# Low parts of the split weights: from a subtraction on VectorE to a negation on ScalarE and an accumulating DMA

## Chip, cores, metric

The kernel runs on one NeuronCore of one Trainium2 chip. The metric is the device time of one launch in microseconds, the median of several runs.

## What is computed

A two-layer decoder trunk on 512 tokens of 1024 channels in float32: one wide input projection, four token mixers (sparse attention NSA, stick-breaking, gated linear attention GLA, forgetting attention FoX), gated branch projections and an output projection, then a feed-forward part with a squared ReLU, and a last norm.

```python
proj = h @ w_in                                   # h = RMSNorm(x), 1024 -> all mixers and gates
ys = jnp.stack([y_nsa, y_sb, y_gla, y_fox], axis=2)
branch = jnp.einsum('bsnc,ncd->bsnd', ys, w_branch)
gates = jax.nn.sigmoid((gate_logits + b_gate).astype(jnp.float32)).astype(x.dtype)
mixed = jnp.sum(gates.reshape(B, S, N_BRANCH, D_MODEL) * branch, axis=2)
x = x + mixed @ w_out
h2 = rms_norm(x, norm_ff)
return x + jnp.square(jax.nn.relu(h2 @ w_ff1)) @ w_ff2
```

## The kernel before

All activations stay on the core, channels on the 128 partitions and the 512 tokens along the row. The weights stream in from device memory in chunks of 128x1024 float32 (512 KB): 350 in the program, in the order in which they are used (`in_w[i]`).

A matrix product is made of three products of a shorter float format (float32r). A weight chunk W is split into a high part `wh` (W rounded to float32r) and a low part W - `wh`; the activations are split likewise into `xh` and `xl`. PE then sums wh*xh + wl*xh + wh*xl. `mtile` (and its kin `mhalves`, `vproducts`) does this: 24 matmuls per chunk, and the second one already uses the low part.

`chunk` (lines 265 to 277) makes the operands. SP loads the chunk into one of three buffers `wr0` to `wr2` (line 271). ACT copies it, rounded, to `wh`, of which there are two buffers (line 275). DVE subtracts `wh` from the raw chunk and writes the low part over the raw chunk (line 276). A `wr` buffer appears under two names: `wr0f` read or written as float32, `wr0r` as float32r. 334 chunks are split this way, 167 per layer: 95 in the mixers, 8 in the output projection, 64 in the feed-forward part. The other 16 (8 per layer, in NSA's compression) are used as they come.

So a `wr` buffer is loaded anew once PE has used the chunk three places earlier, and a `wh` buffer is written anew once PE has used the chunk two places earlier.

In the mixers (some 736 us per layer) a list, `MIXERS`, sets the order in which the pieces of projections and attention are written down, and a scheduler orders the instructions of each engine from there. Attention work lies between the projections' matmuls on PE; POOL does masks (`AFFINE_SELECT`, lines 633 and 713), rotations (line 827) and the sum into `mixed` (line 536). Then comes the output projection (line 465), and the feed-forward part: four groups of 8 chunks that make the hidden tiles (first half: DVE scales by the norm in line 475, ACT squares and rounds in lines 476 and 478, DVE makes the low part in line 479) and 8 chunks that add into `x` (second half, DVE in line 485). Every matmul is recorded at line 121. PSUM tiles are `pd` for the mixers' projections and `ps` elsewhere.

Of the kernel before, what the change touches and what calls it, by code (L numbers as in the profile page):

```python
# [32 lines left out]
# columns of the per-layer small pack  # L33
# [3 lines left out]
# columns of the constant pack  # L37
# [10 lines left out]
class Dual:  # L48
    """a buffer seen as float32 and as float32r"""
# [14 lines left out]
class Kern:  # L64
# [117 lines left out]
    def setup_more(self):  # L182
# [24 lines left out]
        # second-pass key operands: rows 0-63 keys, then rows of -1 (64-95 or 96-127), zeros elsewhere  # L207
# [17 lines left out]
        # rope tables, rows as channels of two heads  # L225
# [29 lines left out]
    def order(self, a, b):  # L255
        """b after a on their engine"""
        self.tc.add_manual_dep(b.ins, a.ins.name,
                               mybir.DependencyInfo(mybir.DependencyClass.NoSync, mybir.DependencyReason.DATA),
                               reason="table order")
# [5 lines left out]
    def chunk(self, split=True):  # L265
        nc = self.nc
        i = self.cidx
        self.cidx += 1
        with self.tc.high_priority(4000 if i == 0 else 2000):
            raw = self.dual("wr")  # L270
            nc.sync.dma_start(raw.f[:], self.A["w"][i])
            if not split:
                return raw.f[:]
            wh = self.t("wh", 1024, F32R)
            nc.scalar.activation(wh[:], raw.f[:], AF.Copy)  # L275
            nc.vector.tensor_sub(raw[:], raw.f[:], fb(wh[:]))  # L276
        return wh, raw

    def mtile(self, xh, xl):
        """one tile of 128 output channels, transposed: [128 ch, 512 tok] in PSUM"""  # L280
        wh, wl = self.chunk()
        o = self.ps(self.dtag)
        n = len(xh)
        for k in range(n):
            s = slice(k * P, (k + 1) * P)
            self.mm(o[:], wh[:, s], xh[k][:], k == 0, False)
            self.mm(o[:], wl[:, s], xh[k][:], False, False)
            self.mm(o[:], wh[:, s], xl[k][:], False, k == n - 1)
        return o

    def mhalves(self, xh, xl):
        """mtile by halves of the tokens: (PSUM, tokens)"""
        wh, wl = self.chunk()
        for h in range(2):
            t = slice(h * 256, h * 256 + 256)
            o = self.ps(self.dtag, 256)
            for k in range(KT):
                s = slice(k * P, (k + 1) * P)
                self.mm(o[:], wh[:, s], xh[k][:, t], k == 0, False)
                self.mm(o[:], wl[:, s], xh[k][:, t], False, False)  # L300
                self.mm(o[:], wh[:, s], xl[k][:, t], False, k == KT - 1)
            yield o, t

    def vproducts(self, bank):
        """256 channels, token-major: two banks of two token tiles"""
        acc = [self.ps(bank) for _ in range(2)]
        for half in range(2):
            wh, wl = self.chunk()
            for k in range(4):
                for t in range(4):  # L310
                    o = acc[t // 2][:, (t % 2) * 256:(t % 2) * 256 + 256]
                    kk = half * 4 + k
                    s = slice(k * 256, (k + 1) * 256)
                    ts = slice(t * P, (t + 1) * P)
                    self.mm(o, self.hh[kk][:, ts], wh[:, s], kk == 0 and t % 2 == 0, False)
                    self.mm(o, self.hl[kk][:, ts], wh[:, s], False, False)
                    self.mm(o, self.hh[kk][:, ts], wl[:, s], False, kk == 7)
        return acc

    def vtiles(self, evac, acc=None):  # L320
        """evac(tok tile, psum [128 tok, 256 ch]) of the next 256 channels"""
        acc = acc or self.vproducts("d")
        with self.hi():
            for t in range(4):
                evac(t, acc[t // 2][:, (t % 2) * 256:(t % 2) * 256 + 256])

# [1 line left out]
    def rms(self, x, bank, early, in_psum=False):  # L328
        """x tiles -> 1/rms per token: [128, 512] (rows alike) and token-major [128, 4]"""
# [33 lines left out]
    def norm_split(self, x, gcol):  # L363
        """x * g as two parts; the tokens' 1/rms goes onto what is made of them"""
        nc = self.nc
        HH, HL = [], []
        for k in range(KT):
            hh, hl = self.hsplit(k)
            g = gcol[:, k:k + 1]
            nc.scalar.activation(hh[:], x[k][:], AF.Copy, scale=g)  # L370
            nc.vector.scalar_tensor_tensor(hl[:], x[k][:], g, fb(hh[:]), OP.mult, OP.subtract)
            HH.append(hh)
            HL.append(hl)
        return HH, HL

    def scaled(self, dst, o, scale=1.0):
        """dst = o * scale / rms"""
# [3 lines left out]
    def final(self, x):  # L381
        """the last norm; the last tile of channels comes in two halves of the tokens"""
# [36 lines left out]
    def layer(self, l, x):  # L419
# [5 lines left out]
        # the first products need no norm before they are written out  # L425
# [25 lines left out]
        # output projection  # L451
# [36 lines left out]
    def ysplit(self, y):  # L488
        """y [128, 512] -> (high, low) tiles; the low part takes y's place"""
# [6 lines left out]
    def sigmoid(self, z):  # L496
        """in place, z at least -44"""
# [5 lines left out]
    def branch(self, n, qt):  # L503
        """mixed += sigmoid(gate_n + b) * (y_n @ W_branch_n), two tiles of channels"""
# [34 lines left out]
    def qk_pair(self, b_tiles=None):  # L539
        """project a pair of heads; per head (A, Q1, Q2) with  # L540
        head 0: A=[kh;kl], Q1=[qh;qh], Q2[0:64]=ql; head 1: A=[kl;kh], Q1=[qh;qh]; with b_tiles
        (rows 0-63 = kh) ql in Q2[0:64], else in the rows of kh"""
# [16 lines left out]
    def kstack(self, k, A, B, b):  # L559
        """k on rows b*64..: its high part there in A, the low part in A's other half"""  # L560
# [7 lines left out]
    def regions(self, S3, win):  # L568
        """per key block: (psum AP, first query)"""
# [13 lines left out]
    def rowmax(self, S3, dst, win, negc=None):  # L583
        """column maxima of the masked scores; dst [32 rows, 512] gets diag(m)"""
# [35 lines left out]
    def probs(self, S3, win=False, bias=None, strict=False):  # L620
        """exp of the scores, masked; list of (AP, first query) per key block"""
# [19 lines left out]
    def pv(self, o, V, pr, start=True):  # L641
        """o [M, 512] += V_j^T P_j"""
# [3 lines left out]
    def recip(self, s, rows):  # L646
        """1/s for s [64 rows of PSUM], written at `rows`"""
# [7 lines left out]
    def v_plain(self, tag, c):  # L655
        """256 channels of values, token-major"""
# [6 lines left out]
    def sb_v(self, c, acc):  # L663
        """values of four heads, each as its high and low parts beside each other"""
# [17 lines left out]
    def sb_att(self, i):  # L682
        """scores with the queries on partitions, so that the sums over later keys are scans"""
# [3 lines left out]
        for b in range(2):  # L687
# [5 lines left out]
            # rows of 128 queries against all keys up to them: (bank, first column)  # L693
# [30 lines left out]
            # keys on partitions: (bank, first column) of a block of keys, queries from the same block on  # L724
# [27 lines left out]
    def vpair_evac(self, V, pair0):  # L752
        """token tile of 256 channels (4 heads) into [V0 | 1 | V1] groups of 192"""
# [15 lines left out]
    def small_proj(self):  # L769
        """nsa gates rows 0-23, gla decay rank rows 32-47, forget gate rows 64-71"""  # L770
# [16 lines left out]
        # gates of the three parts of the sparse attention, through DRAM to be read as rows alike  # L787
# [31 lines left out]
    def rope(self, o, scale, r=None):  # L819
        """rotated o * scale / rms, in r or in a tile of its own"""  # L820
# [11 lines left out]
    def compress_in(self, pecol):  # L832
        """two tiles [128 = (two positions, channel), 8 position pairs, 64 = (group, 31 blocks + pe)]"""
# [22 lines left out]
    def cmp_step(self, i, c):  # L856
        """a quarter of the first compression product"""
# [14 lines left out]
        if c == 3:  # L872
            # the position part
# [74 lines left out]
    def nsa(self, pi):  # L948
        """selected (here: all causal) and window attention of two heads"""
        nc = self.nc  # L950
        g, q, Ab, V = pi // 2, self.q, self.Ab, self.vnsa
        if True:
# [3 lines left out]
            for b in range(2):  # L956
# [7 lines left out]
                for br in range(2):  # L964
# [7 lines left out]
                    # [V|1] or [1|V] by the half the group's values sit in  # L972
# [17 lines left out]
    def nsa_cmp(self, g):  # L990
        """compressed attention of group g's four heads"""
# [40 lines left out]
    def gla_x(self, n, i):  # L1032
        """q (scaled) or k of two heads"""
# [7 lines left out]
    def gla_b(self, i):  # L1041
        """decays of two heads, summed within 64 tokens"""
# [25 lines left out]
    def gla(self, i):  # L1068
# [4 lines left out]
        if True:  # L1073
# [3 lines left out]
            # far pairs: products of decays from the middle of 512, 256 and 128 tokens  # L1077
# [47 lines left out]
            # pairs of one block of two tokens, the diagonal with them  # L1125
# [17 lines left out]
            # the other levels inside a block of 128 tokens; the two heads' queries beside each other,  # L1143
            # each with zeros at the other's channels
# [61 lines left out]
    def logsig(self, z, out):  # L1206
        """out = min(z, 0) - ln(1 + exp(-|z|))"""
# [10 lines left out]
def _kxm(w, c0):  # L1218
    """[K, 128 columns] -> [128, K/128 * 128]"""
    k = w.shape[0] // P  # L1220
    return w[:, c0:c0 + P].reshape(k, P, P).transpose(1, 0, 2).reshape(P, k * P)
# [9 lines left out]
# the token mixers' pieces in the order they are emitted: projections (with weights) and, in steps, attention  # L1231
# [142 lines left out]
```

## Time and profile before

| | |
|---|---|
| median of 3 runs | 2278.51 us (2278.09 to 2279.06) |
| span of the profiled execution | 2273.7 us |
| busy: PE, DVE | 2230.2 us (98%), 1488.2 us (65%) |
| busy: ACT, POOL | 1035.6 us (46%), 428.5 us (19%) |
| DMA traffic | 204.75 MB, mean 90 GB/s |

The profiled execution's span, from its first to its last instruction, is 2273.7 us; the runs' times are some 4.8 us longer. A matmul's row lasts 0.39 us, yet matmuls start every 0.23 us: they are pipelined, so starts tell the beat, and "busy" of PE can hide short waits. PEld is the load of a matmul's weights and runs beside the matmul before it. An idle time in brackets in a timeline names what ended it.

### The profile page before, as it was taken

The page shows a single profiled execution, that of the slowest core. Times are in us where ns is not written, and L with a number is a line of the kernel's source. Part 1 is how long each engine was busy: PE and PEld are TensorE (multiplying, and loading weights), DVE is VectorE, ACT ScalarE, POOL GpSimd, SP SyncE. Part 2 cuts the span into 40 slices and gives each one's busy share as a digit, 9 for nine tenths or more (in the row PEclk, how much of TensorE's full clock was granted, in tenths as well). Part 3 has the DMA queues.
Part 4 walks back from the last instruction along what each step waited for, and adds up shares of the span by engine and source line. Part 5 has one row for each costly group of instructions (what it writes and reads, how often), then busy time and mean ns, then how long its engine had stood idle before and what let it go on. Part 6 is the DMA issues. An engine that isn't in the chain of part 4 may idle for free.

```text
span 2273.7 us, 28986 instructions
## 1 busy us (share of the span) xinstructions
PE 2230.2 (98%) x10740; PEld 1824.9 (80%) x10740; DVE 1488.2 (65%) x2434; ACT 1035.6 (46%) x1663; POOL 428.5 (19%) x759
## 2 busy tenths in 40 slices
PE   8999999999899999999999999999989999999998
PEld 7888878887788888888888888788868888888886
DVE  6889687888875444343458886978888654344344
ACT  5775544445544333232347654534454443232233
POOL 1223024434211200000112220234431112000000
PEclk9999999999999999999999999999999999999999
DMA  4222223322124332333432222233211243333332
GB/s 164 77 72 68 90 68 96 113 79 79 47 67 128 103 93 93 95 99 94 125 105 69 66 75 85 74 98 118 76 56 58 83 130 93 94 99 95 93 94 92
DMA packets 63108, 204.75 MB, mean 90 GB/s; under 512 B 7496, under 2 KB 10184, under 8 KB 62968
## 3 DMA queue, kind: packets, MB, share of 16 engines
q1 hardware_dynamic: 62968, 202.90, 29.1%
q8 instruction: 86, 1.41, 0.3%
q14 instruction: 54, 0.44, 0.1%
HBM read 198.57 MB, written 4.29 MB: 89 GB/s over the span
## 4 chain that ended last, share of the span: by engine, by line
PE 91%; DVE 5%; issue 1%; DMA 1%; ACT 1%; POOL 1%; POOLq 0%; DVEq 0%; SPq 0%; ACTq 0%
PE ps L121 48%; PE pd L121 42%; PE ps L730 1%; DMA wr1f<-in_w 0%; DMA wr0f<-in_w 0%; DVE sh L844 0%; POOL sm L613 0%; DVE wr1r L276 0%; DVE Q L616 0%; DVE m L1214 0%; DVE m L591 0%; DVE sx L609 0%; DVE m L605 0%; DVE Q L1109 0%; ACT wh L275 0%
## 5 line engine op out<-in xcount | busy, mean ns | idle before, releaser
L121 PE MATMUL pd<-hh,wh 128*128 128x512 f32 x1040 | 415.8, 400 | 0.2 <-ACT wh L275 0.2
L121 PE MATMUL pd<-hl,wh 128*128 128x512 f32 x1040 | 407.8, 392 | 0.0
L275 ACT ACTIVATE wh<-wr1f 128x1024 fp32r<-128x1024 f32 x112 | 118.7, 1060 | 274.7 <-PE ps L121 175.0
L275 ACT ACTIVATE wh<-wr0f 128x1024 fp32r<-128x1024 f32 x111 | 117.6, 1060 | 265.4 <-PE ps L121 176.3
L121 PEld LDWEIGHTS pd<-hh,wh 128*128 128x128 f32 x1040 | 195.6, 188 | 50.0 <-issue 4.0
L275 ACT ACTIVATE wh<-wr2f 128x1024 fp32r<-128x1024 f32 x111 | 117.6, 1060 | 256.9 <-PE ps L121 172.7
L121 PEld LDWEIGHTS pd<-hl,wh 128*128 128x128 f32 x1040 | 195.5, 188 | 42.2 <-issue 0.5
L121 PE MATMUL ps<-hh,wh 128*128 128x512 f32 x512 | 201.3, 394 | 0.0
L121 PE MATMUL ps<-hl,wh 128*128 128x512 f32 x512 | 199.3, 389 | 0.0
L276 DVE TENSOR_TENSOR wr0r<-wr0f,wh 128x1024 fp32r<-128x1024 f32 x111 | 143.4, 1292 | 43.0 <-ACT wh L275 42.5
L485 DVE TENSOR_TENSOR x<-x,ps 128x512 f32<-128x512 f32 (+1 forms) x65 | 44.2, 679 | 191.7 <-PE ps L121 191.7
L276 DVE TENSOR_TENSOR wr2r<-wr2f,wh 128x1024 fp32r<-128x1024 f32 x111 | 144.5, 1302 | 35.0 <-ACT wh L275 34.8
L121 PE MATMUL pd<-hh,wr2r 128*128 128x512 f32 x392 | 156.6, 400 | 0.0
L276 DVE TENSOR_TENSOR wr1r<-wr1f,wh 128x1024 fp32r<-128x1024 f32 x112 | 138.1, 1233 | 28.2 <-ACT wh L275 27.7
L475 DVE SCALAR_TENSOR_TENSOR p<-ps,rb 128x512 f32<-128x512 f32 x64 | 43.9, 691 | 157.3 <-PE ps L121 149.2
L121 PE MATMUL ps<-v,wh 128*128 128x512 f32 (+1 forms) x392 | 135.8, 389 | 0.0
L121 PE MATMUL pd<-hh,wr1r 128*128 128x512 f32 x336 | 134.4, 400 | 0.0
L121 PE MATMUL pd<-hh,wr0r 128*128 128x512 f32 x312 | 124.6, 399 | 0.0
L121 PE MATMUL ps<-p,v 128*128 128x384 f32 (+3 forms) x384 | 116.1, 426 | 2.2 <-POOL p L633 2.2
L121 PEld LDWEIGHTS ps<-hh,wh 128*128 128x128 f32 x512 | 96.1, 188 | 24.6 <-issue 0.5
L121 PE MATMUL pd<-yh,wh 128*128 128x512 f32 x256 | 105.0, 410 | 9.9 <-ACT yh L492 9.0
L121 PEld LDWEIGHTS ps<-hl,wh 128*128 128x128 f32 x512 | 96.2, 188 | 21.3
(638 smaller groups left out, 5326.8 us busy)
## 6 DMA issues: line engine op xcount, KB each, us to landing
wr0f<-in_w SPq DMA_DIRECT2D x117, 512.0 KB, 3.6
wr1f<-in_w SPq DMA_DIRECT2D x117, 512.0 KB, 3.6
wr2f<-in_w SPq DMA_DIRECT2D x116, 512.0 KB, 3.6
G<-gd SPq DMA_DIRECT2D x48, 128.0 KB, 3.1
x<-in_x SPq DMA_DIRECT2D x16, 256.0 KB, 3.5
xs<-x SPq DMA_DIRECT2D x8, 256.0 KB, 3.7
x<-xs SPq DMA_DIRECT2D x8, 256.0 KB, 3.3
out_y<-p SPq DMA_DIRECT2D x8, 256.0 KB, 2.4
```

The costliest lines, as they stand in the source:

```text
L121: i = self.nc.tensor.matmul(o, l, r, start=start, stop=stop, skip_group_check=True)
L275: nc.scalar.activation(wh[:], raw.f[:], AF.Copy)
L276: nc.vector.tensor_sub(raw[:], raw.f[:], fb(wh[:]))
L475: nc.vector.scalar_tensor_tensor(r[:], o[:], 0.0, self.rb[:], OP.max, OP.mult)
L485: nc.vector.tensor_add(x[m][:, h], x[m][:, h], o[:])
L730: nc.tensor.transpose(S3[n][:, c:c + P], at(F, q)[:, j * P:(j + 1) * P], self.ident)
```

## The change

The subtraction on DVE goes. ACT writes the negated high part, -`wh`, over the raw chunk (new line 277), and a DMA issued from POOL adds the same chunk of weights from device memory onto it (new line 278): -`wh` + W. The rest of the diff only blanks comments and docstrings, so that lines behind move by two.

```diff
@@ class Kern, chunk() @@
             wh = self.t("wh", 1024, F32R)
             nc.scalar.activation(wh[:], raw.f[:], AF.Copy)
-            nc.vector.tensor_sub(raw[:], raw.f[:], fb(wh[:]))
+
+            nc.scalar.activation(raw[:], fb(wh[:]), AF.Copy, scale=-1.0)
+            nc.gpsimd.dma_start(raw[:], self.A["w"][i].bitcast(F32R), accum_op=OP.add)
         return wh, raw
```

Two places show how the engines' orders move. First ACT, in the first half of the last feed-forward group: `wh` is a chunk's high part, `p` the hidden tile, `v` its rounded high part. Before:

```order
L275 ACTIVATE wh_17453<-wr2f 128x1024
L476 ACTIVATE p_17409<-p_17409 128x512
L478 ACTIVATE v_2216_17412<-p_17409 128x512
L275 ACTIVATE wh_17489<-wr0f 128x1024
L476 ACTIVATE p_17445<-p_17445 128x512
L478 ACTIVATE v_2221_17448<-p_17445 128x512
```

and with the change:

```order
L275 ACTIVATE wh_17738<-wr1f 128x1024
L478 ACTIVATE p_17693<-p_17693 128x512
L277 ACTIVATE wr1r<-wh_17738 128x1024
L480 ACTIVATE v_2211_17696<-p_17693 128x512
L275 ACTIVATE wh_17775<-wr2f 128x1024
L478 ACTIVATE p_17730<-p_17730 128x512
L277 ACTIVATE wr2r<-wh_17775 128x1024
L480 ACTIVATE v_2216_17733<-p_17730 128x512
```

The negation (L277) stands behind the square of a hidden tile (L476 before, L478 now), and the rounding behind the negation.

On POOL, in the stick-breaking pieces of layer 0's mixers (`e0f` to `e5f` are tiles of scores being masked, `qk` a rotated projection). Before:

```order
L713 AFFINE_SELECT e0f<-e0f 128x128
L713 AFFINE_SELECT e1f<-e1f 128x128 x2
L713 AFFINE_SELECT e2f<-e2f 128x128
L713 AFFINE_SELECT e0f<-e0f 128x128
L713 AFFINE_SELECT e1f<-e1f 128x128 x2
L713 AFFINE_SELECT e2f<-e2f 128x128
L827 TENSOR_TENSOR qk_1910<-qk_1910,Sn 128x512
```

and with the change:

```order
L715 AFFINE_SELECT e0f<-e0f 128x128
L715 AFFINE_SELECT e1f<-e1f 128x128 x2
L715 AFFINE_SELECT e0f<-e0f 128x128
L715 AFFINE_SELECT e1f<-e1f 128x128 x2
L278 DMA wr2r<-in_w 128x1024
L715 AFFINE_SELECT e2f<-e2f 128x128
L278 DMA wr0r<-in_w 128x1024
L715 AFFINE_SELECT e2f<-e2f 128x128
L278 DMA wr1r<-in_w 128x1024
L829 TENSOR_TENSOR qk_1932<-qk_1932,Sn 128x512
L278 DMA wr2r<-in_w 128x1024
```

Each adding DMA (L278) has taken a place among the masks, in one queue with them. POOL's list has 342 rows more than before (860 for 518), ACT's 335 more, DVE's 336 fewer, and PE's and SP's as many as they had.

## Rows read from the trace of the kernel before

**Rows 1.** Spans and granted TensorE clock of the cores.

```profile
core 0: 2273.7 us, clock 0.991
```

**Rows 2.** Busy time by stretch: us, busy (xinstructions) per engine, PE clock, DMA share, GB/s.

```profile
core 0: us, PE busy (x) PEld busy (x) DVE busy (x) ACT busy (x) POOL busy (x), PEclk, DMA share, GB/s
300.00:500.00 200.00, 198.74 (x998) 161.47 (x997) 163.91 (x332) 87.29 (x155) 78.63 (x160) 1.00 0.29 89
500.00:700.00 200.00, 189.41 (x922) 151.53 (x921) 159.94 (x287) 100.72 (x168) 50.10 (x68) 0.97 0.23 71
1000.00:1100.00 100.00, 100.00 (x435) 81.46 (x434) 39.78 (x45) 29.04 (x36) 0.00 (x0) 1.00 0.31 97
1400.00:1600.00 200.00, 198.56 (x998) 162.45 (x997) 160.99 (x324) 94.22 (x166) 74.53 (x153) 1.00 0.31 93
1600.00:1800.00 200.00, 189.53 (x921) 149.89 (x920) 167.05 (x310) 96.46 (x164) 55.62 (x87) 0.97 0.21 65
```

**Rows 3.** Chain of waits, two of its longest pieces: start us, us, what.

```profile
671.86 64.25 PE pd L121 x278
...
798.22 344.80 PE ps L121 x1520
```

**Rows 4.** Timeline of PE, first half of the feed-forward part: start us, us, instruction.

```profile
2004.86 0.39 PE L121 MATMUL ps<-hh,wh 128*128 128x512 f32 x1
...
2010.40 0.39 PE L121 MATMUL ps<-hh,wh 128*128 128x512 f32 x1
2010.41 0.19 PEld L121 LDWEIGHTS ps<-hh,wr2r 128*128 128x128 f32 x1
```

**Rows 5.** Timeline of ACT and DVE in the same stretch.

```profile
2005.06 1.06 ACT L275 ACTIVATE wh<-wr2f 128x1024 fp32r<-128x1024 f32 x1 [3.30 <-PE ps L121]
2006.15 1.23 DVE L276 TENSOR_TENSOR wr2r<-wr2f,wh 128x1024 fp32r<-128x1024 f32 x1 [0.40 <-ACT wh L275]
...
2006.67 0.63 ACT L478 ACTIVATE v<-p 128x512 fp32r<-128x512 f32 x1
```

**Rows 6.** Costliest groups, line 276: busy us, mean ns, idle before, what ended it.

```profile
L276 DVE TENSOR_TENSOR wr0r<-wr0f,wh 128x1024 fp32r<-128x1024 f32 x111 | 143.4, 1292 | 43.0 <-ACT wh L275 42.5
...
L276 DVE TENSOR_TENSOR wr1r<-wr1f,wh 128x1024 fp32r<-128x1024 f32 x112 | 138.1, 1233 | 28.2 <-ACT wh L275 27.7
```

**Rows 7.** View of line 276: who waited for it (us, times).

```profile
  PEld pd L121: 3.4, 8
  PE pd L121: 0.8, 2
  PEld ps L121: 0.3, 1
  PE ps L121: 0.3, 1
```

**Rows 8.** Timelines of PE, ACT and DVE, second half of the feed-forward part.

```profile
2049.25 0.39 PE L121 MATMUL ps<-v,wh 128*128 128x512 f32 x1
...
2049.45 1.06 ACT L275 ACTIVATE wh<-wr1f 128x1024 fp32r<-128x1024 f32 x1 [1.95 <-PE ps L121]
...
2050.54 1.22 DVE L276 TENSOR_TENSOR wr1r<-wr1f,wh 128x1024 fp32r<-128x1024 f32 x1 [0.41 <-ACT wh L275]
```

**Rows 9.** DMA: a queue's share; median us to landing; an issue in SP's timeline.

```profile
q1 hardware_dynamic: 62968, 202.90, 29.1%
...
wr0f<-in_w SPq DMA_DIRECT2D x117, 512.0 KB, 3.6
...
G<-gd SPq DMA_DIRECT2D x48, 128.0 KB, 3.1
...
2004.82 0.33 SPq L271 DMA_DIRECT2D wr0f<-in_w  x1
```

**Rows 10.** Waits, one of them: total us, times, longest.

```profile
ACT wh L275 <- PE pd L121: 230.5, 104, 5.4
```

**Rows 11.** Busy time by stretch where PE waits in the mixers (columns as rows 2).

```profile
570.00:580.00 10.00, 4.88 (x20) 3.72 (x18) 9.70 (x18) 7.89 (x15) 4.81 (x4) 0.76 0.00 0
580.00:590.00 10.00, 8.33 (x45) 6.90 (x46) 9.21 (x16) 3.11 (x5) 4.44 (x4) 0.73 0.18 52
```

## Prediction

> **What bounds the kernel now.** The table of spans [rows 1] gives 2273.7 us for the profiled execution at a granted clock of 0.991; the median of the runs is 2278.51, so I add 4.8 us for what lies around the span. The table by stretches [rows 2] says who is busy: from 1000 to 1100 us, in the feed-forward part, PE is busy all the time, DVE 40% and ACT 29%, POOL not at all. In the mixers PE is still at 189 to 199 of 200 us, and DVE at 160 to 167. The chain of waits [rows 3] has the same two faces: one unbroken piece of 344.80 us of PE for the feed-forward part of layer 0 (layer 1 has its like), and in the mixers many pieces of PE, the longest 64.25 us. So PE's matmuls set the time, and anything that PE doesn't wait for is free. The question is whether PE will wait for the new low parts.
>
> The timeline of PE [rows 4] gives the beat. A chunk is 24 matmuls; one begins at 2004.86 and the next at 2010.40, so P = 5.54 us. The second matmul of a chunk already uses the low part, and its weights are loaded at 2010.41. The same chunk's high part is made by ACT at 2005.06, right after the chunk two places earlier has ended at 2004.86, since there are two `wh` buffers, and DVE's low part is done at 2006.15 + 1.23 = 2007.38 [rows 5]: 3.0 us early. That spare time is what the change spends.
>
> **What goes away.** 334 subtractions on DVE, 143.4 us for the 111 of one buffer and 138.1 us for the 112 of another [rows 6], with the third's 144.5 some 426 us in all. In the feed-forward part DVE is not waited for, so this returns nothing there. The low part held up PE's matmuls and weight loads 12 times for 4.8 us in all [rows 7]. In the mixers a freer DVE can give back some of PE's idle time: in the four stretches of rows 2 it is 1.26 + 10.59 + 1.44 + 10.47 = 24 us. Nothing bounds it below but zero, all of it is the upper end, and I take half: **-12 us**.
>
> **What is added on ACT.** 334 negations of 128x1024. ACT's row of the same shape has 1.06 us, so 354 us; ACT is at 29 to 50% in rows 2, and carries the sum. But the negation stands in the path to the low part. In the second half of the feed-forward part a chunk ends at 2049.25, ACT starts the high part at 2049.45, and what read it before started at 2050.54 [rows 8]; the negation starts there and ends at 2051.60, which is 2.35 us after the chunk's end. In the first half the square of the hidden tile stands between the two on ACT (the order of ACT shows it): after the 2005.06 of the high part the next free place is 2006.67 [rows 5], so the negation ends at 2007.73, 2.87 us after the chunk's end. The low part must be there 2010.41 - 2004.86 = 5.55 us after that end. What is left for the transfer is **5.55 - 2.35 = 3.2 us** in the second half and in the output projection, and **5.55 - 2.87 = 2.7 us** in the first half.
>
> **What the accumulating DMA takes, A.** From the end of the negation to the low part's arrival: a hop to POOL, POOL's issue, the transfer with its addition. The trace has no DMA from POOL and none that adds. Low end: a plain load of the same 512 KB takes 3.6 us from issue to landing, median [rows 9]. High end: twice that, 7.2, as if the old value were fetched by a transfer and the sum written by another. Between: the old value has to be read as well, 512 KB more. The hardware queue's packets took 29.1% of 2273.7 us, that is 662 us for 202.90 MB, or 1.7 us for one chunk [rows 9]; 3.6 + 1.7 = 5.3. POOL's issue and the hop I put at 0.7, twice the 0.33 that SP's issue shows [rows 9]. So A = 6.0, nearer to the loads than to two of them in a row, with 3.6 and 7.2 as ends. The Trainium skill, page Collectives: The Full Stack, section The bandwidth ceiling, says that a reducing transfer needs two source reads where a copy needs one, and runs at half the copy's rate for that; with the first read alone A would be 4.3, and the sum below about 200 us smaller. No row here shows it yet.
>
> Even the plain load's 3.6 us misses both places. A lateness of x is paid once in two chunks, not in each: chunk j+2 is late against chunk j, and the chunk between follows j+2 in the same stride. So the loss per chunk is (A - 3.2)/2 or (A - 2.7)/2.
>
> **Feed-forward part and output projection.** Two layers have 2 x (32 + 8) = 80 chunks of the first kind and 64 of the second. 80 x 1.4 + 64 x 1.65 = 112 + 106 = **+218 us**. At A = 3.6 it is 80 x 0.2 + 64 x 0.45 = 45; at 7.2, 160 + 144 = 304.
>
> **Mixers.** 190 chunks, 95 in a layer, in about 736 us (the output projection begins where the 64-us piece that starts at 671.86 ends) [rows 3]. That is 7.7 us per chunk against 5.54, since matmuls of the attention stand between; where they do, the low part has time. In stretches like the 64.25 us (278 matmuls, 11.6 chunks on end) it has none. Working the other way, ACT's high parts here waited for PE's last reader 104 times for 230 us [rows 10], so the ring of two is tight here too; and ACT and POOL serve in order. On POOL the adding DMA waits at the queue's head for ACT, with the attention's masks, rotations and `mixed` sums behind it, which ACT and PE wait for in their turn; and it stands itself behind masks that wait for ACT or DVE. I take half of the 1.4: 190 x 0.7 = **+133 us**. Ends: none of it at A = 3.6 (the attention covers 0.4), 190 x 1.0 = 190 at A = 7.2. SP's loads are moved nowhere: chunk j+3 is still loaded when chunk j ends, lands 3.6 us later, and is needed a chunk later still. The wire carries 334 x 0.52 MB more, 1.7 us of a beat of 5.5, over a share of 0.31 [rows 2]; room enough.
>
> **Sum.** 2273.7 + 218 + 133 - 12 = 2612.7 against the profiled execution; with 4.8 around it, **2618 us**. Changes under 0.2% (4.6 us) count as none.
>
> **Rivals.**
> *A plain load's price.* If adding costs the wire nothing, A lies in 3.6 to 4.8: +45 - 12 and some mixers at the one end, 80 x 0.8 + 64 x 1.05 + 190 x 0.4 - 12 = 195 at the other: 2320 to 2474. For it speaks that the load moves at full width already; against it, that the old value must come from somewhere.
> *PE's clock falls, or the add is slower than 7.2.* The stall of a pair of chunks lies in one piece, about 3 us at A = 6. Where PE stood idle 5 of 10 us, from 570 on, the granted clock was 0.76 and 0.73 in two stretches [rows 11], a mixture of its levels of 1.2 and 2.4 GHz. Losing a quarter of the rate over a pair's 14 us costs 3.5 us, or 1.75 per chunk: 144 x 1.75 = 252, giving 2870. The Trainium skill, page TensorE: Matmul & The Clock Gate, section HAM oscillation, has waits for transfers between bursts of matmuls slow each burst anew; by that rule this rival would hold. Against it: 580 to 590 follows a much emptier stretch. And at A = 9: 80 x 2.9 + 64 x 3.15 + 190 x 1.45 = 709, less 12, giving 2976.
> *Faster.* If the low part arrives within 2.7 us of the negation's end, the feed-forward part loses nothing, and the mixers return up to the 24 us: 2278.5 - 24 = 2255. DVE's load of over 80% in rows 2 is for it. Against it: 2.7 is under the shortest plain load of this size, and under the 3.1 us of one of a quarter of the size [rows 9].
> *The change doesn't do what it says* falls out: the order has 334 negations on ACT, 334 DMAs on POOL and no subtraction of weights on DVE.
>
> **Chances.** Forecast (A from 4.8 to 7.2 with the clock kept, 2474 to 2761) 0.50; plain price 0.15; slower still 0.25; faster 0.06; no change 0.04. The range 2350 to 2930 leaves out faster and no change (0.10), a corner of the plain price (0.02) and the worst of the slow cases (0.08). Slower 0.90, same 0.04, faster 0.06.
>
> **What would show it.** In the feed-forward stretch a chunk should begin every 6.9 to 7.2 us instead of 5.54, with PE waiting in every second chunk at its first low-part matmul for a DMA that POOL issued; that DMA's row should read about 5 us from issue to landing. DVE should fall by 426 us, ACT rise by 354. If PE's beat there stays at 5.54, the transfer fits in 2.7 us and the forecast is wrong in its main term; if PE waits for ACT or a mask rather than for the low part, the mixers' term is.

## The result, and the profile after

The changed kernel takes **2764.34 us** (median of 3 runs, 2762.99 to 2773.08) against 2278.51: **1.2145 times as long, interval 1.2119 to 1.217**. The forecast was 2618 with a range of 2350 to 2930; the sign and the main mechanism held, and the size fell 146 us short of the time. The forecast's own case, an adding transfer of at most 7.2 us with the clock kept, ended at 2761; that the range held the result by a wide margin it owes to the rival of the clock.

First the table of spans (as [rows 1]): the profiled execution grew by 487.5 us, and the granted clock fell.

```profile
core 0: 2761.2 us, clock 0.952
```

If the clock is always at one of its two levels, 2.4 and 1.2 GHz (full and half), a mean of 0.952 means 2 x 0.048 x 2761.2 = 265 us at half clock, where before had 2 x 0.009 x 2273.7 = 41.

The view of DMA (as [rows 9]) shows the new queue and its transfers; the last number of an issue's row is the median from issue to landing.

```profile
q0 software_dynamic: 48096, 175.13, 39.2%
q1 hardware_dynamic: 62968, 202.90, 22.9%
...
wr0f<-in_w SPq DMA_DIRECT2D x117, 512.0 KB, 3.7
...
wr1r<-in_w POOLq DMA_DIRECT2D x112, 512.0 KB, 5.6
```

The adds move less than the loads, and take more of the 16 DMA engines: 0.392 x 2761.2 / 334 = 3.24 us for a chunk, against 1.6 us for a loaded one, worked out in the same way.

Now the timelines in the first half of the feed-forward part, as [rows 4, 5], for one chunk. ACT:

```profile
1050.62 1.06 ACT L275 ACTIVATE wh<-wr1f 128x1024 fp32r<-128x1024 f32 x1 [4.12 <-PE ps L121]
1051.58 0.61 ACT L478 ACTIVATE p<-p 128x512 f32<-128x512 f32 x1
1052.10 1.04 ACT L277 ACTIVATE wr1r<-wh 128x1024 fp32r<-128x1024 f32 x1
1053.05 0.62 ACT L480 ACTIVATE v<-p 128x512 fp32r<-128x512 f32 x1
1057.61 1.06 ACT L275 ACTIVATE wh<-wr2f 128x1024 fp32r<-128x1024 f32 x1 [3.94 <-PE ps L121]
```

POOL:

```profile
1053.44 0.86 POOL L278 DMA_DIRECT2D wr1r<-in_w  x1 [6.29 <-ACT wr1r L277]
```

PE:

```profile
1057.41 0.40 PE L121 MATMUL ps<-hh,wh 128*128 128x512 f32 x1
1059.04 0.47 PE L121 MATMUL ps<-hh,wr1r 128*128 128x512 f32 x1 [1.23 <-ACT wh L275]
1059.34 0.40 PE L121 MATMUL ps<-hl,wh 128*128 128x512 f32 x1
```

The negation ends at 1053.14, the add's row starts 0.30 later, and this transfer lands at 1058.94, after 5.5 us; PE takes up the first low product at 1059.04. The bracket there names ACT's high part, but that row (the first of ACT's) had ended at 1051.68: a wait for several semaphores is put down to one of them, and the time shows that it was the transfer. The others are alike: all 182 first low products for which PE stood idle over 0.15 us (79 in the mixers, 103 behind them) start 0.04 to 0.09 us after their own chunk's add has landed. PE's chunk takes 1057.61 - 1050.62 = 6.99 us by ACT's starts, instead of 5.54. A wait costs a little more than its bracket: from 1057.41 to 1059.04 are 1.63 us where the beat is 0.23, and the next start comes 0.07 late too, so 1.47 for a bracket of 1.23, or 0.24 on top in this wait.

PE's idle time before matmuls that read a low part is grouped by operand (`pd` the mixers' tiles, `ps` here the first half's of the feed-forward part; busy us, mean ns, idle before). In the same six groups before, it was 0.0.

```profile
L121 PE MATMUL pd<-hh,wr2r 128*128 128x512 f32 x392 | 166.8, 426 | 46.7 <-DMA wr2r<-in_w 14.5 <-ACT wh L275 9.3 <-issue 6.6
L121 PE MATMUL pd<-hh,wr1r 128*128 128x512 f32 x336 | 139.7, 416 | 29.1 <-DMA wr1r<-in_w 8.6 <-ACT wh L275 8.5 <-issue 4.7
L121 PE MATMUL pd<-hh,wr0r 128*128 128x512 f32 x312 | 129.4, 415 | 25.0 <-DMA wr0r<-in_w 14.3 <-ACT wh L275 4.5 <-ACT A L565 3.0
...
L121 PE MATMUL ps<-hh,wr1r 128*128 128x512 f32 x176 | 73.4, 417 | 25.1 <-ACT wr2r L277 12.1 <-ACT p L478 6.6 <-ACT wh L275 4.8
L121 PE MATMUL ps<-hh,wr0r 128*128 128x512 f32 x168 | 70.3, 418 | 26.2 <-ACT wr1r L277 13.3 <-ACT p L478 7.2 <-ACT wh L275 5.0
L121 PE MATMUL ps<-hh,wr2r 128*128 128x512 f32 x168 | 70.1, 417 | 25.7 <-ACT p L478 6.9 <-ACT v L480 5.9 <-ACT wr0r L277 4.2
```

Summed over all groups that read a low part, by their place on PE's timeline, this is 138 us in 85 waits in the mixers and 175 us in 109 waits in the output projection and feed-forward part.

Last the stretches (columns as [rows 2]): two of the mixers, and the output projection with the feed-forward part of each layer.

```profile
300.00:500.00 200.00, 178.22 (x750) 139.36 (x751) 99.29 (x216) 98.13 (x147) 63.88 (x127) 0.94 0.59 130
500.00:700.00 200.00, 179.58 (x899) 144.05 (x898) 128.63 (x299) 102.61 (x175) 84.55 (x148) 0.92 0.54 124
854.10:1378.90 524.80, 432.60 (x1741) 332.38 (x1740) 85.51 (x125) 200.41 (x243) 81.23 (x87) 0.97 0.68 148
2209.90:2761.20 551.30, 446.85 (x1798) 346.13 (x1797) 93.90 (x149) 203.57 (x248) 76.40 (x84) 0.94 0.65 142
```

DVE is relieved as foreseen (99 for 164 us in the first, where PE gets through 750 matmuls and not 998), PE waits everywhere, and the clock is below 1 in all four. In this table and below, a layer is cut where ACT starts the first high part (L275) of the output projection (the layer's 96th split chunk) and where the next layer begins. "Mixers" is what lies before the first cut, "rest" (output projection and feed-forward part) what lies behind it; both are summed over the two layers of the profiled execution, in us. The times of e3, e4, e5, e7, e8 and e9 are of one run each, the others medians of several.

| kernel | time | mixers | rest |
|---|---|---|---|
| before | 2278.51 | 1453 | 821 |
| the change | 2764.34 | 1685 | 1076 |
| low products last (e1) | 2394.68 | 1517 | 876 |
| before, low products last (e2) | 2299.46 | 1474 | 824 |
| change in the mixers only (e3) | 2518.72 | 1692 | 824 |
| change in the rest only (e4) | 2561.35 | 1454 | 1105 |
| copying instead of adding (e5) | 2488.72 | 1563 | 924 |
| before, ACT's high part twice (e6) | 2341.37 | 1493 | 845 |
| waits filled with matmuls (e7) | 2749.97 | 1673 | 1075 |
| change in the rest, 3 `wh` buffers (e8) | 2491.22 | 1517 | 972 |
| later waits filled (e9) | 2728.52 | 1674 | 1052 |
| four chunks a layer only (e10) | 2279.63 | 1457 | 821 |
| before, a POOL DMA per chunk (e11) | 2276.96 | 1458 | 821 |
| before, no low part (e12) | 2263.72 | 1443 | 817 |

The mixers lost 232 us and the rest 255. The kernel before took 2274.2 to 2277.1 us beside these runs.

### The profile page after: what moved, and what is told of

It is laid out like the page before. It is cut to its first block, busy times and chain, and to the rows that moved or that the text cites. A ratio compares the mean times of both kernels' runs of the same rounds, so it can differ in the third digit from the quotient of the medians.

```text
span 2761.2 us, 30120 instructions
## 1 busy us (share of the span) xinstructions
PE 2374.7 (86%) x10740; PEld 1884.3 (68%) x10740; DVE 1080.7 (39%) x2100; ACT 1354.6 (49%) x1997; POOL 676.1 (24%) x1093
## 4 chain that ended last, share of the span: by engine, by line
PE 65%; DMA 11%; issue 10%; ACT 9%; DVE 4%; POOL 1%; POOLq 0%; SPq 0%; DVEq 0%; ACTq 0%
PE ps L121 33%; PE pd L121 32%; ACT wh L275 4%; DMA wr0r<-in_w 3%; DMA wr2r<-in_w 2%; DMA wr1r<-in_w 2%; DMA wr0f<-in_w 1%; DMA G<-gd 1%; ACT wr0r L277 1%; ACT wr2r L277 1%; DMA wr2f<-in_w 1%; ACT wr1r L277 1%; ACT hh L372 0%; PE ps L732 0%; DMA wr1f<-in_w 0%
## 5 line engine op out<-in xcount | busy, mean ns | idle before, releaser
L121 PE MATMUL pd<-hh,wh 128*128 128x512 f32 x1040 | 427.6, 411 | 4.6 <-ACT wh L275 3.1
L121 PE MATMUL pd<-hl,wh 128*128 128x512 f32 x1040 | 423.7, 407 | 0.0
L275 ACT ACTIVATE wh<-wr1f 128x1024 fp32r<-128x1024 f32 x112 | 118.7, 1060 | 370.4 <-PE ps L121 220.9
L275 ACT ACTIVATE wh<-wr2f 128x1024 fp32r<-128x1024 f32 x111 | 117.7, 1060 | 343.4 <-PE ps L121 224.6
L275 ACT ACTIVATE wh<-wr0f 128x1024 fp32r<-128x1024 f32 x111 | 117.6, 1059 | 342.9 <-PE ps L121 219.6
L121 PEld LDWEIGHTS pd<-hl,wh 128*128 128x128 f32 x1040 | 204.8, 197 | 43.8 <-issue 1.7
L278 POOL DMA_DIRECT2D wr1r<-in_w x112 | 97.4, 870 | 536.4 <-ACT wr1r L277 512.0
L278 POOL DMA_DIRECT2D wr2r<-in_w x111 | 96.7, 871 | 476.8 <-ACT wr2r L277 454.5
L121 PE MATMUL pd<-hh,wr2r 128*128 128x512 f32 x392 | 166.8, 426 | 46.7 <-DMA wr2r<-in_w 14.5
L278 POOL DMA_DIRECT2D wr0r<-in_w x111 | 96.8, 872 | 444.4 <-ACT wr0r L277 440.1
L121 PE MATMUL ps<-v,wh 128*128 128x512 f32 (+1 forms) x392 | 144.3, 411 | 8.2 <-ACT wh L275 8.2
L121 PEld LDWEIGHTS pd<-hh,wr2r 128*128 128x128 f32 x392 | 78.1, 199 | 72.5 <-DMA wr2r<-in_w 15.8
L277 ACT ACTIVATE wr1r<-wh 128x1024 fp32r<-128x1024 f32 x112 | 118.3, 1056 | 1.8
```

The source lines that it names most:

```text
L121: i = self.nc.tensor.matmul(o, l, r, start=start, stop=stop, skip_group_check=True)
L277: nc.scalar.activation(raw[:], fb(wh[:]), AF.Copy, scale=-1.0)
L278: nc.gpsimd.dma_start(raw[:], self.A["w"][i].bitcast(F32R), accum_op=OP.add)
```

## The experiments

### Is it the low part's lateness?

**e1**, the change with the low products of a chunk behind its high ones, so that the low part is due 16 matmuls later; `mhalves`, `vproducts` and the branch products alike. **e2** is the same order without the change.

```diff
@@ def mtile() @@
             self.mm(o[:], wh[:, s], xh[k][:], k == 0, False)
-            self.mm(o[:], wl[:, s], xh[k][:], False, False)
-            self.mm(o[:], wh[:, s], xl[k][:], False, k == n - 1)
+            self.mm(o[:], wh[:, s], xl[k][:], False, False)
+        for k in range(n):
+            s = slice(k * P, (k + 1) * P)
+            self.mm(o[:], wl[:, s], xh[k][:], False, k == n - 1)
```

> The changed kernel, with PE's matmuls of a chunk in another order: its 16 high-part products first, its 8 low-part products last. Theory (the low part's 5.9 us from the negation's end is what PE waits for): the low part is now needed 16 x 0.23 = 3.7 us into the chunk, and the high buffer is free 8 x 0.23 = 1.8 us before the chunk's end, so the room for the transfer grows from 2.7 to 3.2 us to over 8 us; feed-forward part and output projection return from 1076 to 821 us, and the mixers give back most of their 232 us: 2280 to 2320 us. Rival (in the mixers it is ACT's and POOL's fuller queues, whatever the low part's date): feed-forward part back, mixers not: about 2510 us. Rival (PE's clock keeps the loss): no such quick return, over 2600 us.

> The kernel before with the same new order of PE's matmuls, as a control: DVE's low part was 3.0 us early in the feed-forward part, so a later need gains nothing there; theory: 2278 us within 0.5%. If the new order by itself were worth something in the mixers (the high buffers free earlier), it shows here, up to 24 us.

e1 took 2394.68 us, 1.053 (1.0514 to 1.0546) of before, e2 2299.46, 1.0111 (1.0094 to 1.0128). The control e2 is itself a small miss: it was expected within 0.5% of before, and lost 21 us in the mixers. The new order gives back 370 of the 486 us. It moves the low part's due date, and also frees the high part's buffer 8 matmuls earlier; either way the path has more room, so most of the loss is the wait for the low part. The rest is not nothing: e1 stays 95 us above e2, which was not expected. Some 78 of them are still waits for low parts, and the transfers point to why these come later (view of DMA, then of the stretch 1000 to 1100):

```profile
q0 software_dynamic: 48096, 175.13, 44.1%
...
wr1f<-in_w SPq DMA_DIRECT2D x117, 512.0 KB, 4.1
...
wr1r<-in_w POOLq DMA_DIRECT2D x112, 512.0 KB, 7.0
```

```profile
1000.00:1100.00 100.00, 97.20 (x419) 77.95 (x418) 17.96 (x26) 45.61 (x50) 15.33 (x18) 1.00 0.84 184
```

Once PE's beat is back near 5.9 us, the DMA engines are at 0.84, the add lands after 6.6 to 7.0 us and the load after 4.1 to 4.2, and ACT's high part waits for loads:

```profile
ACT wh L275 <- DMA wr0f<-in_w: 156.3, 59, 8.3
```

**e5**, the change with a copy in place of the add.

```diff
-            nc.gpsimd.dma_start(raw[:], self.A["w"][i].bitcast(F32R), accum_op=OP.add)
+            nc.gpsimd.dma_start(raw[:], self.A["w"][i].bitcast(F32R))
```

> The changed kernel with POOL's DMA copying the chunk instead of adding it: the sum is left out, so the low part is replaced by the whole weight. Theory (the add costs a second read, 1.5 to 1.7 us on the wire): from issue to landing about 4.0 us instead of 5.6, so A is 4.3; by the prediction's terms the loss falls from 487 to about 487 - 200 = 290 us or less: 2450 to 2560 us. Rival (the price is POOL's way of issuing, and the add is free): landing 5.6 us as now and 2764 us.

It took 2488.72 us:

```profile
q0 software_dynamic: 48096, 175.13, 24.5%
...
wr1r<-in_w POOLq DMA_DIRECT2D x112, 512.0 KB, 3.9
```

So the addition itself costs 5.6 - 3.9 = 1.7 us of the path, and 276 us of the time. On the DMA engines the copy takes 0.245 x 2487.0 / 334 = 1.82 us for a chunk, the add 3.24. The rest shrank by 152 us: 144 chunks x 1.7 / 2 = 122 by the prediction's rule, and the time at half clock there fell from 98 to 24 us.

**e8**, the change in the rest only, with a third `wh` buffer (`r` and `qk` give one up), to break the rule that a lateness is paid every second chunk.

```diff
-    TAGS = dict(wh=(2, 1024), yh=(5, 512), gt=(2, 512), v2=(4, 512), v3=(4, 768), A=(5, 512), Q1=(3, 512),
-                Q2=(2, 512), m=(2, 512), r=(3, 512), p=(4, 512), sh=(3, 512), sm=(5, 64), sx=(6, 16), ng=(4,
-                32), bc=(6, 1), rb=(1, 512), rt=(1, 4), hid=(1, 256), qk=(3, 512), G=(2, 512))
+    TAGS = dict(wh=(3, 1024), yh=(5, 512), gt=(2, 512), v2=(4, 512), v3=(4, 768), A=(5, 512), Q1=(3, 512),
+                Q2=(2, 512), m=(2, 512), r=(2, 512), p=(4, 512), sh=(3, 512), sm=(5, 64), sx=(6, 16), ng=(4,
+                32), bc=(6, 1), rb=(1, 512), rt=(1, 4), hid=(1, 256), qk=(2, 512), G=(2, 512))
```

> The accumulating DMA in the output projection and feed-forward part alone (2561 us, 1105 us there), with three buffers for the high part; two tags that the mixers use give up one buffer each for the room. Theory (two high buffers put the whole path between the end of one chunk and the second next): the path may now take two chunks; what binds next is the ring of three raw buffers, load 3.9 + two ACT passes and square 2.7 + 5.9 to 7.3 us + the chunk's 5.3, over three: 5.9 to 6.4 us a chunk, 144 of them 850 to 920 us: about 2310 to 2390 us. Rival (the wire is full): 7 us a chunk stays.

A miss: 2491.22 us. The rest fell from e4's 1105 to 972 us, but to no less, and the new buffer counts cost the mixers 63 us against e4. ACT hardly waits for PE's last reader of `wh` any more, but for loads:

```profile
ACT wh L275 <- DMA wr0f<-in_w: 257.9, 92, 8.1
```

A `wr` buffer now goes through load (4.1, median in the rest), high part and negation (2.1), add (6.7) and PE's use (5.5) before it can be loaded again: 18.4 us for three buffers is a beat of 6.1 at least, by these medians; the rest's mean is 972 / 144 = 6.75. The next ring behind the one relieved was as short.

### Where, and what else the change brings

**e3** and **e4**, the change in one part of each layer alone (`i % 175 < 103` and `>= 103`), DVE subtracting elsewhere.

```diff
+            if i % 175 < 103:
                 nc.scalar.activation(raw[:], fb(wh[:]), AF.Copy, scale=-1.0)
                 nc.gpsimd.dma_start(raw[:], self.A["w"][i].bitcast(F32R), accum_op=OP.add)
+            else:
+                nc.vector.tensor_sub(raw[:], raw.f[:], fb(wh[:]))
```

> The accumulating DMA for the mixers' chunks alone; in the output projection and the feed-forward part DVE subtracts as before. Theory (each part pays for itself): 2764 - 255 = 2509 us. Rival (the feed-forward part's loss comes from elsewhere, as from the clock): above 2600 us.

> The accumulating DMA for the chunks of the output projection and the feed-forward part alone. Theory: 2764 - 232 = 2532 us, a beat of 7.0 to 7.5 us per chunk there, mixers as before at 731 and 722 us. Rival (the mixers' loss spills over): another sum.

2518.72 and 2561.35 us: each part loses by itself. The mixers lose the same as in the whole (1692 for 1685), the rest 29 us more (1105 for 1076), for which the clock answers below.

**e6**, before with ACT's high part made twice, for the longer work on ACT.

```diff
+            nc.scalar.activation(wh[:], raw.f[:], AF.Copy, scale=-1.0)
             nc.scalar.activation(wh[:], raw.f[:], AF.Copy)
```

> The kernel before (DVE subtracts), with one more ACT pass over each chunk: ACT writes the negated high part into the high buffer and then the high part over it, 334 x 1.06 us more on ACT and both parts 1.1 us later. Theory (ACT has room, the date of the low part is what counts and DVE is early by more than that): 2275 to 2310 us. Rival (the mixers lose by ACT's fuller queue): 2400 us or more, with the feed-forward part unchanged at 5.54 us a chunk.

A miss: 2341.37 us, 1.0291 (1.0274 to 1.0308). It delays the high part by 1.06 us, which the change does not; still it shows that 1.06 us of delay on this path costs 66 us, of them 40 in the mixers. As much work on ACT as the change adds thus cost the mixers 40 us here, delay included, where the change cost them 232.

**e11**, before with a DMA of 4 KB per split chunk on POOL, which waits for ACT as the change's does.

```diff
             nc.vector.tensor_sub(raw[:], raw.f[:], fb(wh[:]))
+            nc.gpsimd.dma_start(self.t("dm", 8, F32R)[:], wh[:, 0:8])
```

> Edit: the kernel before, DVE subtracting as ever, and one more DMA per split chunk, issued from POOL, that waits for ACT's high part like the change's DMA does and copies 8 columns of it to a tile that nobody reads. It brings the change's place at the head of POOL's queue and POOL's issue, without any wait of PE for a transfer. Theory (the mixers lose by the late low parts and by the clock, not by POOL's masks and sums standing behind the DMAs): 2274 to 2285, mixers 731 to 735 us a layer against 730.6 and 722.4. Rival (POOL's order is a good part of the 232 us that the mixers lost): 2320 or more, mixers 750 or more, PE waiting for masks or for the branch sums.

2276.96 us, 1.0 (0.9991 to 1.001). POOL issued 334 of them, and the time did not move: in a kernel where PE does not wait, the place in POOL's queue, ahead of masks and sums, is free. (POOL's row is 0.53 us here, 0.87 for the adds, so 0.34 us of the occupation is not covered by this.) The changed kernel's own trace has the other side, POOL's work ahead of the adds: of the 79 waits in the mixers above, 9 are for an add that POOL issued 1.2 to 2.1 us after the negation's end and not 0.3, which makes 12 us of lateness together. ACT began the negations of these 79 on the mean 0.6 us after the high part's end.

**e12**, before without the low parts.

```diff
-            nc.vector.tensor_sub(raw[:], raw.f[:], fb(wh[:]))
-        return wh, raw
+        return wh, wh
```

> Edit: the kernel before without the low parts: no subtraction, no DMA in its place, and the matmuls that read a low part read the high part a second time (the low parts' share of the products is left out, and wrong weights are added for it). The matmuls are as many as before. It prices the relief of DVE alone, a term that the prediction took as 12 us between 0 and 24. Theory: 2255 to 2272, all of it in the mixers, where PE's idle time falls. Rival (PE's idle time in the mixers is the attention's own chain, which a freer DVE does not shorten, as the four-chunk version suggests): 2273 to 2280, that is no change.

2263.72 us, 0.9954 (0.9939 to 0.9968): 11.6 us less than its before, some 10 of it in the mixers. DVE's relief is worth what the prediction took, at most: the edit also frees the `wr` buffers early.

**e10** tried to cash this in: the adding DMA for four chunks of a layer alone, where DVE is busiest and PE idle [rows 11].

```diff
+            if i % 175 in (79, 80, 81, 82):
                 nc.scalar.activation(raw[:], fb(wh[:]), AF.Copy, scale=-1.0)
                 nc.gpsimd.dma_start(raw[:], self.A["w"][i].bitcast(F32R), accum_op=OP.add)
+            else:
+                nc.vector.tensor_sub(raw[:], raw.f[:], fb(wh[:]))
```

> Edit: the adding DMA for four split chunks of each layer alone (positions 79 to 82 of the 175), which are spaced 8 to 23 us apart in the mixers and where DVE is about 95% busy while PE has idle gaps; DVE subtracts in all the others. Theory (the longer path costs only where chunks follow each other faster than it lasts; where they do not and DVE ends the waits, taking a subtraction from DVE is worth up to 1.6 us a chunk): 2264 to 2275, a gain of 0 to 5 us a layer. Rival (nothing waits for DVE there, or the work is dealt out otherwise): 2274 to 2285.

2279.63 us, 1.0019 (1.001 to 1.0028), a little slower. From 560 to 580 us, before and then with this edit:

```profile
560.00:580.00 20.00, 12.24 (x42) 8.74 (x40) 19.25 (x53) 14.01 (x28) 10.53 (x13) 0.79 0.13 41
```

```profile
560.00:580.00 20.00, 11.96 (x47) 8.95 (x45) 15.05 (x45) 14.78 (x30) 6.50 (x11) 0.79 0.40 86
```

DVE has 4 us less to do, and PE is as idle as before. But it is not the same idleness. In each layer two of the four adds were still late, by 0.3 and 1.4 us; the first layer's are these:

```profile
554.50 0.47 PE L121 MATMUL pd<-hh,wr1r 128*128 128x512 f32 x1 [0.32 <-ACT wh L275]
...
562.74 0.47 PE L121 MATMUL pd<-yh,wr2r 128*128 128x512 f32 x1 [1.38 <-ACT sx L1100]
```

The adds had landed at 554.41 and 562.65, 0.09 us before each. From 545 to 605 us PE's other waits fell from 9.4 to 7.4 us, and 1.7 us of waits for adds took their place. So a freer DVE does give back some 2 us here, and the longer path takes nearly as much; where the other 4 us of the kernel's time went is open. Of the versions that compute all of it, none beats the kernel before.

### The clock

PE's timeline behind two waits of the changed kernel, nearly alike in length:

```profile
1193.19 0.47 PE L121 MATMUL ps<-hh,wr2r 128*128 128x512 f32 x1 [2.88 <-ACT yl5r L480]
...
2376.85 0.77 PE L121 MATMUL ps<-yh,wr2r 128*128 128x512 f32 x1 [2.92 <-ACT wr0r L277]
...
2379.55 0.63 PE L121 MATMUL ps<-yh,wr2r 128*128 128x512 f32 x1
2379.98 0.63 PE L121 MATMUL ps<-yl0r,wh 128*128 128x512 f32 x1
2380.40 0.63 PE L121 MATMUL ps<-yl1r,wh 128*128 128x512 f32 x1
```

Behind the second, matmuls start every 0.43 us and not every 0.23: half clock. The chain of waits has the price, for 47 matmuls each (those behind the wait of 1193.19, then the next wait's, then those behind 2376.85):

```profile
1193.19 11.10 PE ps L121 x47
...
1207.14 11.07 PE ps L121 x47
...
2376.85 13.92 PE ps L121 x47
```

**e7** fills PE's waits in the rest with five matmuls whose result nobody reads; **e9** does so only behind the first group of eight.

```diff
             self.mm(o[:], wh[:, s], xh[k][:], k == 0, False)
+            if k == 0 and self.dtag == "s" and self.cidx % 175 > 119:
+                z = self.ps("d")
+                for _ in range(5):
+                    self.mm(z[:], wh[:, s], xh[k][:], True)
```

(e7 is without the condition on `cidx`.)

> The changed kernel with five more matmuls per chunk in the output projection and the feed-forward part, into an unused PSUM tile, between the first high-part product and the first low-part product: 1.15 us of work in a gap of some 1.5 us, so that PE stands idle less. Theory (the gaps also cost clock, 255 us lost where the prediction's sum at full clock has 218): granted clock near 1.0 there, and output projection plus feed-forward part fall from 1076 towards 1039 us: 2720 to 2750 us. Rival (the clock costs nothing): no shorter, 2764 us or up to 40 us more, since the gaps are not all as long as the filling.

> Edit: the change, and five more matmuls (into a tile of their own) ahead of the first low product, only in the chunks of the feed-forward part behind its first group of eight. Theory (a part of the feed-forward loss is TensorE's half clock, not the wait alone, 0.2 to 0.3 us a chunk by the later groups of the run with all gaps filled): the stall is filled rather than shortened, the half-clock time of the part falls, and feed-forward and output projection of both layers together fall from 1076 us to 1046 to 1060; in all 2735 to 2750. Rival (the wait on the low part alone sets the beat, or the five matmuls cost what the clock gives back): 1070 to 1080, in all about 2764.

e7 gave 2749.97 us, with the rest unchanged (1075): its first group of eight takes 8.8 us a chunk instead of 7.5, and its later ones are mostly quicker than the change's, so its time decided nothing. e9 gave 2728.52, with the rest at 1052, in the theory's interval; the time is below it, for the mixers, which the edit leaves alone, came out 11 us shorter. The stretches of the rest, e9's first and then e4's:

```profile
840.10:1357.30 517.20, 483.02 (x2014) 377.33 (x2013) 85.50 (x125) 200.42 (x243) 81.20 (x87) 0.99 0.68 151
2191.30:2726.50 535.20, 489.06 (x2073) 383.95 (x2072) 93.90 (x149) 203.57 (x248) 76.39 (x84) 0.98 0.66 146
```

```profile
731.90:1268.10 536.20, 440.05 (x1740) 341.52 (x1739) 85.48 (x125) 200.19 (x243) 81.25 (x87) 0.94 0.66 145
1990.50:2559.30 568.80, 460.94 (x1798) 359.54 (x1797) 93.90 (x149) 203.39 (x248) 76.35 (x84) 0.91 0.62 137
```

Time at half clock is 2 x (1 - clock) x length: 32 us in e9, 98 in the change, 167 in e4, for 1052, 1076 and 1105 us. That is 24/66 and 29/69, or 0.36 to 0.42 us lost per us at half clock, with matmuls added to the change in e9 and with none in e4. A microsecond at half clock can cost 0.5 at most.

These are single runs, but PE's starts give the price inside each. Take every interval from one matmul's start to the next, less the median for the same two shapes in the kernel before. The intervals that begin at half clock and hold no wait (no idle time over 0.1 us) add up, in the rest, to 10 us more than before in e9, 38 in the change, 66 in e4: the differences, 28 us each, are most of what the three times differ by (24 and 29). In e7 they add up to 9. So its filling did return the clock's 29 us; but the added matmuls and the waits left over took 37 us more than the waits that they filled.

## Why the prediction was right, and what it left out

**The path.** A, from the negation's end to the landing, was put at 6.0 us and is 0.3 + 5.6 = 5.9. The second read was to cost 1.7, and e5 has 1.7; issue and hop were to cost 0.7, and a copy from POOL has 0.3 + 3.9 against the load's 3.6, so 0.6. The Trainium skill, page Collectives: The Full Stack, section The bandwidth ceiling, has a reducing transfer read two sources and run at half the copy's rate. The traces agree roughly: the add takes 3.24 us of the DMA engines and e5's copy 1.82, that is 1.8 times, but only 1.4 times the copy's time to landing.

**The loss for a given A.** The rule of half a lateness per chunk held at full clock. The stretch shown above has a wait of 1.2 us in each chunk, others one of 2.6 to 2.9 in every second, and both give a beat of 7.0 (1050.62 to 1057.61, and 1207.14 - 1193.19 = 13.95 for two); the prediction had 6.9 to 7.2. With that 0.24 us, read from one wait, on top of each bracket, the waits for low parts come to 175 + 109 x 0.24 = 201 us in the rest, where 218 were predicted, and 138 + 85 x 0.24 = 158 in the mixers, where 133 were: 359 for 351.

**DVE's relief**, 12 us, is e12's 11.6 at most. POOL's queue, which the mixers' term named beside ACT's, costs nothing that e11 could show; the change's trace has the 12 us of late adds above for it, and among PE's other waits in the mixers those that POOL ended are 4 us for 2 before.

**What failed: "with the clock kept", and PE's other waits.** The forecast took the loss in waits for low parts alone, less DVE's relief, and left the clock to a rival. The clock did fall: 265 us at half clock for 41, of which the rest has 98 for 9, and the mixers 167 for 32. Counted from PE's starts as above, the intervals at half clock cost 87 us more than before (49 in the mixers, 38 in the rest). Those that end in a wait for a low part cost 346 more, the small lengthenings that are left 18, and those that end in any other wait 35, where PE was to wait 12 less; by brackets these other waits grew from 36 to 67. Together 486 of the 487.5 that were lost. The forecast had 218 + 133 - 12 = 339, so of the 148 that it was short, 87 are the clock, 47 the other waits, and some 13 the waits for low parts. That these two terms were left out is what failed, and the sum came as near as it did because the waits for low parts are the greater part. In the rest the clock's price is shown (e9, and e4 beside the change); in the mixers it is counted in one trace, and no run took it away. Of the other waits in the mixers, those that DVE ended grew from 12 to 27 us, although DVE had less to do; what held DVE up there was not followed up.

**The rival of the clock was mis-sized too.** It had a quarter of the rate lost everywhere, 252 us in the rest alone, where 38 were lost. The Trainium skill, page TensorE: Matmul & The Clock Gate, section HAM oscillation, on which it leaned, has every burst behind a transfer's wait start slow, in an example whose waits are mostly longer than those here. The trace agrees for some bursts and not for others: after 2.92 us of waiting at 2376.85 the burst ran at half clock, after 2.88 us at 1193.19 at full. Forecast and rival were each half right, and adding a part of the rival's price to the forecast would have been nearer than choosing. What decides between two such waits stays open.

**"Room enough" on the wire** was right only because the stall made room: the prediction had 1.7 us of the wire for each chunk, where the add takes 3.24, and at the change's beat of 7 us the DMA share is 0.65 to 0.68. With the beat near the old one the share is 0.84, and adds and loads both land later (e1): the term takes the place of the first one as soon as that is cured.

**Off in size only:** ACT rose by 319 us for 354 (its rows overlap by 0.1 us, as at 1051.58 above), DVE fell by 407.5 for 426. The adds' rows have 5.6 us for "about 5". Of the 4.8 us that were put around the span, the changed kernel's run shows 1.8 (2762.99 for a span of 2761.2); the rest is the difference between executions.

## What to carry to other kernels

Before work is moved off an engine that has time to spare, add up the new path from the release of its input to its first reader, and compare it with the slack at that reader: here 5.9 us of transfer went into a gap of 2.7 to 3.2. Then price the waits twice, once as time and once for the clock, and take the second as a share and not as all or nothing. When a ring is lengthened or an order changed to hide a long path, work out the next ring and the wire at the beat that is hoped for, not at the stalled one.

## What was not expected of the hardware

- An adding transfer keeps the DMA engines twice as long as a load of the same 512 KB (3.24 us a chunk for 1.6), and in e1, with the DMA engines at 0.84, both land later: 6.6 to 7.0 us for 5.6, and 4.1 to 4.2 for 3.7.
- POOL's row for each such issue lasts 0.87 us (median), where SP's has 0.33 [rows 9]; for 4 KB it was 0.53 (e11).
- Of two waits of 2.9 us, one left the clock at full (1193.19) and one at half (2376.85).
